# An add and a tanh-GELU over 1024 x 4096: the first load of x as eight transfers of sixteen rows

## The chip, the cores and the metric

The kernel runs on one core of a Trainium2 chip. The metric is the device time of one execution in microseconds (us), as the median of three runs. Beside it there is one profiled execution, from which every view of the profile below is taken. The profile gives times from the first instruction of the program; the span ends with the last one that it shows.

## The reference

```python
def setup_inputs():
    batch, dim = 1024, 4096
    return {"x": randn(batch, dim) as float32, "y": randn(batch, dim) as float32}

def reference(x, y):
    z = x + y
    return (0.5 * z * (1 + np.tanh(np.sqrt(2 / np.pi) * (z + 0.044715 * z ** 3)))).astype(np.float32)
```

Two arrays of 16.8 MB each are read, one of 16.8 MB is written, and every element takes one addition and one GELU. No matrix product occurs.

## The kernel before

**Layout.** The 1024 x 4096 array is viewed as 128 partitions of 8 rows each (`xv`, `yv`, `ov`, line 91), so that one partition holds 32768 consecutive floats, 128 KB. The partition is therefore the outer index of the DRAM side too: neighbouring partitions lie 128 KB apart in DRAM. The tile `zt` (line 120) holds all of x, is overwritten in place by z = x + y and at last by the result. Two buffers `y` of 8192 columns (32 KB in each partition) hold y in turn.

**Transfers.** All are issued on the SP engine's one queue. x comes in two loads of 16384 columns (`xloads`, 64 KB in each partition, 8.4 MB each), y in four loads of 8192 columns (4.2 MB each), and three stores of 16384, 10240 and 6144 columns follow. The order written out in `sp` (lines 173 to 176) is x0, y0, y1, x1, y2, y3 and then the stores. y2 may be issued only when the adds that read y0 have ended, since it takes that buffer, and y3 likewise after the adds on y1. The first store has a hand-made wait on chunk 8 (`FIRST`, line 138).

**Compute.** The columns are cut in 16 chunks of 2048. For each chunk `add` (line 149) runs on GpSimd (POOL) or on VectorE (DVE) as the table `by_dve` says; `mag` (line 154) writes the absolute value into PSUM on ScalarE (ACT); `gelu` (line 157) applies the GELU to the negated absolute value there; `end` (line 166) adds max(z, 0) on VectorE. The last is the identity gelu(z) = max(z, 0) + gelu(-|z|). The order on every engine is written out by hand (lines 173 to 211).

**Beginning and end.** After the program is compiled, `begin_early(nc, count)` takes the first `count` transfers of the SP engine out of the body and puts them ahead of the program's opening barrier, at the very head of SP's stream; with `count` 2 these are x0 and y0. It asserts that none of them waits for anything. `wait_late` lets the final barrier go on without the last store's semaphore and puts one wait for it at the end, on ScalarE.

**Semaphores of transfers.** The framework gives the transfers semaphores in turn from a set of eight (DMAHW0 to DMAHW7). The kernel before issues nine transfers: x0 has DMAHW0, y0 DMAHW1, y1 DMAHW2, x1 DMAHW3, y2 DMAHW4, y3 DMAHW5, the stores DMAHW6, DMAHW7 and, once more, DMAHW0. A transfer that takes a semaphore again waits until the earlier transfer with it has landed.

Of the kernel before, what the change touches and what calls it, by code (L numbers as in the profile page):

```python
# [8 lines left out]
def begin_early(nc, count):  # L9


    head, body = (b.instructions for b in nc.main_func.blocks[:2])
    SP = mybir.EngineType.SP
    moved = [i for i in body if i.engine == SP and isinstance(i, mybir.InstDMACopy)][:count]
    assert not any(i.sync_info and i.sync_info.on_wait for i in moved)
    assert all(i.regs_accessed() == ((), ()) for i in moved)
    at = next(k for k, i in enumerate(head) if i.engine == SP)
    for k, i in enumerate(moved):
        body.remove(i)
        head.insert(at + k, i)  # L20


def wait_late(nc):

    body, end = (b.instructions for b in nc.main_func.blocks[1:3])
    last = [i for i in body if isinstance(i, mybir.InstDMACopy)][-1]
    (sem,) = [u.id for u in last.sync_info.on_update]
    all_done = end[0]  # L30
    reset = next(i for i in end if isinstance(i, mybir.InstDrain) and i.is_reset_sema)
    at = end.index(reset)
    clear = end[at + 1]
    first, stop = reset.reset_range_start, reset.reset_range_stop
    assert all_done.engine == mybir.EngineType.SP and reset.engine == mybir.EngineType.Pool
    assert isinstance(clear, mybir.InstISA) and clear.engine == mybir.EngineType.Pool
    waits = all_done.sync_info.on_wait
    (its,) = [w for w in waits if w.id == sem]

    end[0] = mybir.InstDrain(  # L40
        name=all_done.name, engine=all_done.engine, debug=all_done.debug, is_reset_sema=False,
        sync_info=mybir.SyncInfo(on_wait=[w for w in waits if w.id != sem], on_update=[]),
    )
    parts = []
    for f, e in ((first, sem), (sem + 1, stop)):
        if f < e:
            nc.gpsimd.sem_clear(range(f, e))
            parts.append(nc.cur_bb.bb.instructions.pop())
    end[at + 1 : at + 2] = parts
    end.append(  # L50
        mybir.InstEventSemaphore(
            name=clear.name, engine=mybir.EngineType.Activation, debug=clear.debug,
            sync_info=mybir.SyncInfo(
                on_wait=[its],
                on_update=[
                    mybir.SyncUpdate(
                        sync_type="semaphore", id=sem, ant_name=its.ant_name,
                        update_mode="sem-sub-imm", update_value=its.wait_value,
                    )
                ],  # L60
            ),
        )
    )
# [3 lines left out]
def kernel(  # L67
# [11 lines left out]

    nc = tc.nc
    P = nc.NUM_PARTITIONS
    fp32 = mybir.dt.float32
# [6 lines left out]
    xv, yv, ov = (a.rearrange("(p n) d -> p (n d)", p=P) for a in (x, y, out))  # L91
# [28 lines left out]
    zt = pool_sb.tile([P, TOT], fp32, tag="z", name="z")  # L120
    yt, wt, ends = {}, {}, {}

    def load_x(i):
        a, b = xr[i]
        nc.sync.dma_start(out=zt[:, a:b], in_=xv[:, a:b])  # L125

    def load_y(i):
        a, b = yr[i]
# [45 lines left out]
    for i, (a, b) in enumerate(xr):  # L174
        sp += [(load_x, i)] + [(load_y, j) for j, (c, _) in enumerate(yr) if a <= c < b]
# [3 lines left out]
    for c in range(C):  # L179
# [6 lines left out]
            (add, c) for c in over(cr, yr[i][0] - 2 * YS, yr[i][1] - 2 * YS)  # L186
        ],
        add: lambda c: [(load_x, i) for i in over(xr, *cr[c])]
        + [(load_y, i) for i in over(yr, *cr[c])],
        mag: lambda c: [(add, c)] + ([(end, c - PS)] if c >= PS else []),  # L190
# [22 lines left out]
    ctx.close()  # L213
    tc.close()
    tc.compile()  # L215
    begin_early(nc, 2)
    wait_late(nc)


# [28 lines left out]
```

## Time and profile before

| | |
|---|---|
| median of three runs | 120.34 us (120.29 to 120.54) |
| the profiled execution's own time | 120.27 us |
| its span | 118.8 us |
| VectorE, ScalarE, GpSimd busy | 59.8, 60.8, 55.5 us |
| bytes read and written | 33.55 and 16.78 MB |

The span is 1.47 us shorter than the time of the same execution; the rest lies around it. In what follows, a "releaser" is what ended a wait; "landing" is the moment at which a transfer's semaphore has its full count; the digits of the slice rows are tenths of 40 equal slices of the span, 2.97 us each.

### The profile page before, as it was taken

The page shows a single profiled execution, that of the slowest core. Times are in us where ns is not written, and L with a number is a line of the kernel's source. Part 1 is how long each engine was busy: PE and PEld are TensorE (multiplying, and loading weights), DVE is VectorE, ACT ScalarE, POOL GpSimd, SP SyncE. Part 2 cuts the span into 40 slices and gives each one's busy share as a digit, 9 for nine tenths or more (in the row PEclk, how much of TensorE's full clock was granted, in tenths as well). Part 3 has the DMA queues.
Part 4 walks back from the last instruction along what each step waited for, and adds up shares of the span by engine and source line. Part 5 has one row for each costly group of instructions (what it writes and reads, how often), then busy time and mean ns, then how long its engine had stood idle before and what let it go on. Part 6 is the DMA issues. An engine that isn't in the chain of part 4 may idle for free.

```text
span 118.8 us, 160 instructions
## 1 busy us (share of the span) xinstructions
DVE 59.8 (50%) x24; ACT 60.8 (51%) x34; POOL 55.5 (47%) x14
## 2 busy tenths in 40 slices
DVE  0000000000399999699994595257999457742000
ACT  5000000000057989999369804797798999940000
POOL 0000000000399999998000029999999999200000
DMA  9899988989999988998899999998899889999895
GB/s 353 353 419 596 397 353 364 497 375 463 419 430 452 530 353 375 640 397 353 353 463 419 452 430 397 474 541 353 375 640 397 353 353 441 441 441 441 381 422 257
DMA packets 1296, 50.33 MB, mean 424 GB/s; under 512 B 144, under 2 KB 144, under 8 KB 144
## 3 DMA queue, kind: packets, MB, share of 16 engines
q1 hardware_dynamic: 1296, 50.33, 98.5%
HBM read 33.55 MB, written 16.78 MB: 424 GB/s over the span
## 4 chain that ended last, share of the span: by engine, by line
DMA 48%; POOL 33%; POOLq 4%; ACT 3%; DVE 2%; issue 0%; SPq 0%; DVEq 0%
DMA y<-in_y_dram 48%; POOL z L149 33%; POOLq L215 4%; DVE z L166 2%; ACT w L154 2%; ACT w L157 2%; SPq L125 0%; POOLq L149 0%; DVEq L166 0%
## 5 line engine op out<-in xcount | busy, mean ns | idle before, releaser
L149 POOL TENSOR_TENSOR z<-z,y 128x2048 f32<-128x2048 f32 x10 | 55.3, 5560 | 45.9 <-DMA y<-in_y_dram 45.9
L154 ACT ACTIVATE w<-z 128x2048 f32<-128x2048 f32 x16 | 30.1, 1880 | 42.8 <-DVE z L149 36.3
L166 DVE SCALAR_TENSOR_TENSOR z<-z,w 128x2048 f32<-128x2048 f32 (+1 forms) x17 | 36.3, 2156 | 16.0 <-ACT w L157 16.0
L149 DVE TENSOR_TENSOR z<-z,y 128x2048 f32<-128x2048 f32 x6 | 24.0, 4009 | 30.6 <-DMA y<-in_y_dram 30.6
L157 ACT ACTIVATE w<-w 128x2048 f32<-128x2048 f32 x16 | 29.8, 1862 | 0.5
L200 ACT ACT_TABLE_LOAD x1 | 1.3, 1283 | 1.3 <-PEq L232 1.3
L199 DVE MEMSET one<- 128x1 f32 x1 | 0.1, 59 | 1.3 <-PEq L232 1.3
L200 ACT ACTIVATE one<-one 128x1 f32<-128x1 f32 x1 | 0.2, 203 | 0.0
L232 POOL MEMSET const-float32-0.0<- 128x1 f32 x1 | 0.1, 99 | 0.2 <-issue 0.2
L232 POOL MEMSET const-bfloat16-1.0<- 128x1 bf16 x1 | 0.1, 102 | 0.0
L232 POOL MEMSET const-uint8-127<- 128x1 uint8 x1 | 0.1, 102 | 0.0
L232 POOL MEMSET const-float32-1.0<- 128x1 f32 x1 | 0.1, 99 | 0.0
## 6 DMA issues: line engine op xcount, KB each, us to landing
y<-in_y_dram SPq DMA_DIRECT2D x4, 4096.0 KB, 28.3
out_dram<-z SPq DMA_DIRECT2D x1, 5120.0 KB, 14.9
out_dram<-z SPq DMA_DIRECT2D x1, 3072.0 KB, 10.9
z<-in_x_dram SPq DMA_DIRECT2D x2, 40.5
out_dram<-z SPq DMA_DIRECT2D x1, 21.6
```

The lines of the kernel that those rows point to most:

```text
L149: eng.tensor_add(out=zt[:, a:b], in0=zt[:, a:b], in1=yt[s][:, o : o + b - a])
L154: nc.scalar.activation(out=wt[c], in_=zt[:, a:b], func=act.Abs)
L157: nc.scalar.activation(out=wt[c], in_=wt[c], func=act.Gelu_apprx_tanh, scale=-1.0)
L166: ins = nc.vector.scalar_tensor_tensor(out=zt[:, a + o : a + o + n], in0=zt[:, a + o : a + o + n], scalar=0.0, in1=wt[c][:, o : o + n], op ...
L199: nc.vector.memset(one, 0.0)
L200: nc.scalar.activation(out=one, in_=one, func=act.Gelu_apprx_tanh)
L215: tc.compile()
L232: nc = _bacc.Bacc("TRN2", target_bir_lowering=False, num_devices=1)
```

## The change

The load x0 of 128 partitions becomes eight loads of 16 partitions. Load j takes the partitions j, j+8, j+16, ..., j+120, each with the same 64 KB of columns as before. The second load of x is left as it was. `begin_early` now takes eight transfers to the head of SP's stream, which are these eight; y0 stays in the body, behind the opening barrier.

```diff
     def load_x(i):
         a, b = xr[i]
-        nc.sync.dma_start(out=zt[:, a:b], in_=xv[:, a:b])
+        for r in [slice(j, P, 8) for j in range(8)] if i == 0 else [slice(0, P)]:
+            nc.sync.dma_start(out=zt[r, a:b], in_=xv[r, a:b])
...
-    begin_early(nc, 2)
+    begin_early(nc, 8)
```

In the changed program's SP stream the eight loads stand first, on DMAHW0 to DMAHW7. Then come the opening barrier and y0, which takes DMAHW0 again and so waits for load 0 of x; y1 takes DMAHW1 and waits for load 1, x1 takes DMAHW2 and waits for load 2. The loads y2 and y3 and the stores keep their places and their waits on the compute engines. The first addition on each engine waits for all eight semaphores in place of two. The order of instructions on VectorE, ScalarE and GpSimd is otherwise the same.

## The prediction

> **What bounds the kernel now.** I read the slice rows first, then the list of queues, the chain, and at last stretches of the span.
>
> The page's rows for DMA (share of the 16 DMA engines, rate by slice, packets) and its queue list:
>
> ```profile
> DMA  9899988989999988998899999998899889999895
> GB/s 353 353 419 596 397 353 364 497 375 463 419 430 452 530 353 375 640 397 353 353 463 419 452 430 397 474 541 353 375 640 397 353 353 441 441 441 441 381 422 257
> DMA packets 1296, 50.33 MB, mean 424 GB/s; under 512 B 144, under 2 KB 144, under 8 KB 144
> q1 hardware_dynamic: 1296, 50.33, 98.5%
> ```
>
> The engines that move data are occupied from the first slice to the last, 98.5% of the span; no compute engine passes 51%. The packet count tells how a transfer is cut: nine transfers x 16 engines = 144 tiny packets, one semaphore update for each engine and transfer, and 1296 - 144 = 1152 = 9 x 128, so one packet for each partition row: 64 KB in x. A slice of 353 GB/s is 16 packets of 65536 bytes booked at their start in 2.97 us; the unevenness of the row is that booking.
>
> The chain that ended last, in order of time (start, length, what):
>
> ```profile
> 0.00 0.38 SPq L125
> 0.38 0.05 issue
> 0.43 31.17 DMA y<-in_y_dram
> ...
> 44.92 25.47 DMA y<-in_y_dram
> ```
>
> The chain names y, but y0 stands on the same rings behind x0, so its 31.17 us are mostly x0's. The rates of four stretches (start:end, length, engines busy, clock, DMA share, GB/s), in x0, in y0, and in both later halves:
>
> ```profile
> 3.00:20.00 17.00, 0.00 (x0) 0.00 (x0) 0.00 (x0) 1.00 1.00 432
> 22.00:31.00 9.00, 0.00 (x0) 0.00 (x0) 0.00 (x0) 1.00 1.05 451
> 42.00:60.00 18.00, 17.00 (x7) 14.86 (x9) 13.97 (x3) 1.00 1.00 431
> 80.00:98.00 18.00, 13.87 (x5) 15.91 (x10) 18.00 (x5) 1.00 0.94 408
> ```
>
> Loads at 431 to 451, whether compute runs or not: 432 / 16 = 27 GB/s for each engine, and 65536 B / 27 = 2.42 us for one row. The packet records of the trace say the same: each of 16 streams has rows of 2.418 to 2.422 us back to back, from about 1.0 us to 118.3 us, except its first, of 2.6 to 3.5 us. What each engine must move is fixed, so whatever x0 loses or gains at its engines reaches the end one for one, unless a queue runs dry, which none does now.
>
> [...]
>
> **The change part by part.**
>
> [...]
>
> *Price of x0.* Before: 8 rows x 2.42 = 19.4 us on each engine. After: 8 x 4.84 = 38.7 us. That is +19.4 us. [...] The first rows end between 3.86 and 4.66 us in the packet records, so D is 0 to 0.8; I take 0.25, -0.5. [...]
>
> *Seven more semaphore updates on each engine.* In the packet records the row after an update starts 6 ns after it. 7 x 6 = 0.04 us on the path.
>
> *Start of the first rows.* [...] Before, first packets start at 1.01 to 1.52 us. The last could start earlier by up to 0.5 us, or nothing could change; the slow engine sets the end, so -0.4 to 0. Most of it is the same lead D as above, so I count it nothing further.
>
> *The eight issues and the barrier.* Issues of loads took 0.33 to 0.50 us on SP; eight are about 3.1 us. A row takes at least 2.42 us, an issue 0.4, so the rings stay fed. The opening barrier comes some 2.3 us later (3.1 us of issues against 0.38 + 0.42), so ScalarE's table load moves from 1.26 to about 3.6. The first addition comes at 31.7, which hides it with 28 us to spare. Cost 0.
>
> *The new waits on SP.* y0 waits for load 0, which lands about 1 + 5.4 + 0.5 = 7 us; behind it stand y1 (load 1, some 12 us) and x1 (load 2, some 17 us). The rings hold x0 until about 40 us by then, 20 us by the old rate. Cost 0; y0 would have to come 13 us later than expected before an engine ran dry. The first additions' six extra waits are met long before y0 lands. y2 and y3 wait for additions which shift as a whole with y0 and y1: before, y2 was issued at 44.9, 15 us ahead of its place in the rings (x1 landed at 1.6 + 59.0 = 60.6), and that lead stays. The stores' hand-made wait shifts likewise. So nothing absorbs the loss, since compute was waiting for data, and the tail after y3 is the old one.
>
> *Sum.* +19.4 - 0.5 + 0.04 = +18.9 us. Against the profiled execution: span 118.8 + 18.9 = 137.7, plus 1.47 around it = 139.2; against the median, 120.34 + 18.9 = 139.3. I predict 139.3.
>
> **The rivals.**
>
> *The ports don't bind.* The pace is the engine's own: 27 GB/s is what an engine shows here[...]. [...] For it: the change then leaves every row at 2.42 us. [...] Then the effect is at the start: up to -0.4 us where the stagger of first packets goes, +0.04 for updates. 120.0, not slower; from -0.24 us it counts as faster. It decides as soon as the rows of x0 keep 2.42 us.
>
> [...]
>
> *Row pitch in HBM alone.* [...] No run here shows it.
>
> That the change does not do what it says is out: the order of the changed program has the eight loads at the head.
>
> **How the numbers follow.** Half the ports with even service: 0.85, from 137.8 (D = 0.8 and some start) to 141.6 [...], which holds it 0.95 of the time. Ports that don't bind: 0.08, half of it faster and half the same. Uneven service 0.04, pitch alone 0.03, both slower. 0.85 x 0.95 = 0.81, so the range is the likeliest case's own. No change means within 0.2%, 0.24 us, about what a measurement of this kernel can tell. Faster 0.04, same 0.04, slower 0.92.
>
> **What would show it.** [...] first addition at about 50.6 us rather than 31.7; y0's issue near 7 us; later stretches equal to the old, 19 us later. It is wrong if the stretch from 3 to 20 us still shows 432, or if the first addition stays at 31.7; and if the rate is halved but a stretch with idle engines follows, a wait on SP cost what I called nothing.

## The result, and the profile after

| | before | after |
|---|---|---|
| median, same chip, four runs each | 120.31 us (120.28 to 120.54) | 142.01 us (141.83 to 142.26) |
| profiled execution: time, span | 120.27, 118.8 us | 141.83, 140.1 us |

The ratio is 1.180, with a 95% interval of 1.1777 to 1.1824: 21.7 us slower. The forecast was slower, 139.3 us with a range of 137.8 to 141.6, so the direction and the place were right and the size too small by 2.7 us.

The same rows of the page as before, now of the changed kernel (share of the 16 DMA engines, rate by slice of 3.5 us, packets, queue):

```profile
DMA  9909909949938999999969699999969696899897
GB/s 299 281 19 299 299 0 299 299 94 206 299 94 356 449 449 440 412 496 393 505 299 599 299 449 440 421 430 402 552 299 599 299 599 299 374 491 444 377 407 302
DMA packets 1408, 50.33 MB, mean 359 GB/s; under 512 B 256, under 2 KB 256, under 8 KB 256
q1 hardware_dynamic: 1408, 50.33, 98.6%
```

The engines are as occupied as before (98.6% against 98.5%), and yet move 359 GB/s in place of 424. An occupied transfer engine need not be a fast one. The first twelve slices show 16 rows (299 GB/s) starting and then often a slice with nothing starting; the zeros in the DMA row come from the same booking at a packet's start. From the thirteenth slice on the rates are the old ones. The packets have grown by 112 = 7 x 16, the seven more semaphore updates on each engine: those under 512 B are 256 in place of 144.

The chain that ended last, in order of time (start, length, what):

```profile
0.00 7.98 DMA z<-in_x_dram
7.98 0.02 issue
8.00 44.90 DMA y<-in_y_dram
...
66.15 25.53 DMA y<-in_y_dram
```

y0 is now issued at 8.00, when load 0 has landed, and lands at 52.90 in place of 31.60. The second long piece is 25.53 us against 25.47 before. So everything is lost ahead of y0's landing: 21.3 us there, 21.3 us in the span.

Stretches of the changed kernel (start:end, length, three engines busy, clock, DMA share, GB/s). The first is cut so that exactly six rows of each engine start in it; the others lie in y0, x1 and the stores' part:

```profile
7.50:38.17 30.67, 0.00 (x0) 0.00 (x0) 0.00 (x0) 1.00 1.00 205
42.00:50.00 8.00, 0.00 (x0) 0.00 (x0) 0.00 (x0) 1.00 0.99 418
62.00:80.00 18.00, 17.00 (x7) 16.08 (x9) 15.18 (x3) 1.00 0.98 422
100.00:118.00 18.00, 14.12 (x6) 15.87 (x10) 18.00 (x4) 1.00 1.08 466
```

x0 runs at 205 GB/s, and what follows at full rate. In the packet records a row of 64 KB takes 5.11 us on every engine, where it took 2.42. The first stretch was made as long as six such rows, so its rate says the same as the row: 16 x 65536 B in 5.11 us are 205 GB/s.

SP's queue in the changed kernel (start, length, line, count):

```profile
0.00 5.00 SPq L127 DMA_DIRECT2D z<-in_x_dram  x8
8.00 5.45 SPq L134 DMA_DIRECT2D y<-in_y_dram  x2
18.23 0.33 SPq L127 DMA_DIRECT2D z<-in_x_dram  x1
```

y0, y1 and x1 wait as the semaphores say, yet all are issued by 18.6 us, while rows of x0 (what the prediction calls the rings are the rows that wait their turn) go on until 42.6 us. These waits cost nothing.

### The profile page after: what moved, and what is told of

Read it like the earlier page. It is cut to its first block, busy times and chain, and to the rows that moved or that the text cites. A ratio compares the mean times of both kernels' runs of the same rounds, so it can differ in the third digit from the quotient of the medians.

```text
span 140.1 us, 179 instructions
## 1 busy us (share of the span) xinstructions
DVE 59.8 (43%) x24; ACT 60.8 (43%) x34; POOL 55.5 (40%) x14
## 3 DMA queue, kind: packets, MB, share of 16 engines
q1 hardware_dynamic: 1408, 50.33, 98.6%
## 4 chain that ended last, share of the span: by engine, by line
DMA 56%; POOL 28%; POOLq 3%; ACT 3%; DVE 2%; issue 0%; DVEq 0%
DMA y<-in_y_dram 50%; POOL z L151 28%; DMA z<-in_x_dram 6%; POOLq L217 3%; DVE z L168 2%; ACT w L156 1%; ACT w L159 1%; DVEq L168 0%; POOLq L151 0%
```

## The experiments

The theory under test is that the rate of a load follows from the SBUF partitions that its rows go to. The prediction and the expectations speak of ports for this (port theory); that was an assumption, and no trace of this case shows a port. Three rivals: the rows' distance in DRAM (pitch theory), a loss at the end of every transfer (transfer theory), and the move of y0 behind the barrier with its waits. Only x0's load is edited, unless it says otherwise, and the edits are shown against the changed kernel, the last one against the kernel before. Where a version ran once, its single time stands beside the median (or the single time) of before on the same chip; the differences of time read from such runs are over 20 us.

**Sixteen neighbouring partitions.**

```diff
-        for r in [slice(j, P, 8) for j in range(8)] if i == 0 else [slice(0, P)]:
+        for r in [slice(16 * j, 16 * j + 16) for j in range(8)] if i == 0 else [slice(0, P)]:
```

> Load j of x0 takes partitions 16j to 16j+15 in place of j, j+8, ...; still eight loads of sixteen rows, rows now 128 KB apart in DRAM. Port theory: [...] a row of 64 KB takes 4 x 2.42 to 4 x 2.56 = 9.7 to 10.2 us, x0 77 to 82 us, time about 178 to 183 us. HBM pitch theory (rows 1 MB apart are what is slow): the pitch is an eighth, rows near 2.42 us, time about 120.5 us. Transfer theory (a row followed by its own semaphore update is slow, wherever it goes): rows 5.11 us as in the changed kernel, time about 142 us.

174.63 us (before 120.18). The stretch of six rows of this run:

```profile
11.00:66.30 55.30, 0.00 (x0) 0.00 (x0) 0.00 (x0) 1.00 1.00 114
```

114 GB/s, about a quarter of the full 432, and a row takes 9.22 us. A loss that grows with the rows' distance, and one that comes with each transfer's end, are both out: rows lie nearer in DRAM and the transfers are as many, and it is 33 us slower than the change. The port theory's direction holds; its size, 178 to 183, rested on an assumed fourfold row (9.7 to 10.2 us) and was a little too high.

**Near in DRAM, far in SBUF.** Load j reads sixteen neighbouring rows and writes them 8 partitions apart. The second half of x and all of y are as they were.

```diff
+            to = slice(0, P) if j is None else slice(j, P, 8)
+            of = slice(0, P) if j is None else slice(16 * j, 16 * j + 16)
-            nc.sync.dma_start(out=zt[r, a:b], in_=xv[r, a:b])
+            nc.sync.dma_start(out=zt[to, a:b], in_=xv[of, a:b])
```

> Load j of x0 reads rows 16j to 16j+15 of x, 128 KB apart in DRAM, and writes them to partitions j, j+8, ..., so x stands in other partitions than y and the output is another function of the inputs; the work is the same. Port theory: only the side of SBUF counts, rows 5.11 us, time 142 us. HBM pitch theory: rows near 2.42 us, about 120.5 us. Transfer theory: 142 us.

141.58 us (before 120.18). The stretch of six rows:

```profile
7.50:38.17 30.67, 0.00 (x0) 0.00 (x0) 0.00 (x0) 1.00 0.99 205
```

The rate of the change again, with another source layout: the side of SBUF decides. Rows take 5.085 us in place of 5.11. That half a percent can't be put down to the pitch, for the rows of the versions below that also run at 205 or 206 GB/s differ as much (5.06 to 5.12 us), and not in the order of their pitch.

**Eight loads of all partitions.** The same number of transfers, with the same waits and y0 in the same place, but cut along the columns.

```diff
-        for r in [slice(j, P, 8) for j in range(8)] if i == 0 else [slice(0, P)]:
-            nc.sync.dma_start(out=zt[r, a:b], in_=xv[r, a:b])
+        w = 2048 if i == 0 else b - a
+        for o in range(a, b, w):
+            nc.sync.dma_start(out=zt[:, o : o + w], in_=xv[:, o : o + w])
```

> x0 as eight loads of all 128 partitions and 2048 columns: the same number of transfers, semaphores and waits, the same place of y0 behind the barrier[...]. Port theory: x0 runs at 27 GB/s for each engine, 120.3 us give or take 0.6 for the beginning. HBM pitch theory: the pitch is that of before, 120.3 us. Transfer theory: eight times a loss at each transfer's end, of up to 2.7 us each, up to 142 us. If the new waits on SP were what costs, 142 us too.

120.67 us against 120.18, ratio 1.0037 (1.0023 to 1.0052), and x0 at the old rate:

```profile
5.00:19.50 14.50, 0.00 (x0) 0.99 (x2) 0.00 (x0) 1.00 1.01 426
```

Number of transfers, semaphores, waits and barrier together are worth some 0.5 us (0.3 to 0.6) of the 21.7, and the 8 KB rows, 0.309 us each or 2.47 for 64 KB, have part of it.

**Four loads of 32 partitions, 4 apart.**

```diff
-        for r in [slice(j, P, 8) for j in range(8)] if i == 0 else [slice(0, P)]:
+        for r in [slice(j, P, 4) for j in range(4)] if i == 0 else [slice(0, P)]:
...
-    begin_early(nc, 8)
+    begin_early(nc, 4)
```

> x0 as four loads of 32 partitions j, j+4, j+8, ...[...]. Port theory, [...] rows 2.42 us, 120.3 us give or take 0.6. Port theory, if an engine takes two neighbours of the list (j+8e, then j+8e+4): [...] rows 5.11 us, 142 us. [...] Transfer theory (half as many transfers): about 131 us.

120.52 us, ratio 1.0031 (1.0021 to 1.0042). The stretch in x0:

```profile
5.00:19.50 14.50, 0.00 (x0) 0.00 (x0) 0.00 (x0) 1.00 1.00 434
```

So a step in the partitions need not cost: this step of 4 over the whole range has 434 GB/s, where the step of 8 had 205. Full rate also says that an engine is not given two neighbours of the list, j+8e and j+8e+4, in that order on all engines at once, since sixteen rows j+8e are a load of the change, which ran at 205 GB/s. Already the first rows take 2.93 to 3.39 us, much as before the change (2.63 to 3.50); which engine takes which row the trace does not say. The first packets start at 1.33 to 1.65 us in place of 1.01 to 1.52, and the last row of x0 ends 0.21 us later.

**Two other sets of sixteen.** Two runs ask whether the 5.11 us belong to the step of 8. First a step of 4 inside a half of 64 (the rows of a load lie 512 KB apart in DRAM):

```diff
-        for r in [slice(j, P, 8) for j in range(8)] if i == 0 else [slice(0, P)]:
+        for r in [slice(h + j, h + 64, 4) for h in (0, 64) for j in range(4)] if i == 0 else [slice(0, P)]:
```

> x0 as eight loads of sixteen partitions with a step of 4 inside one half of 64 (j, j+4, ..., j+60, then 64 more)[...] and rows read together lie 512 KB apart[...]. Port theory: slow all the same, near 142 us. [...] rows 5.11 us, 142 us. [...] rows 4.61 us[...], x0 4 us shorter, 138 us. [...] HBM pitch theory: 120.5 us.

141.21 us (before 120.24), rows 5.06 us. Then a step of 2 inside a quarter of 32:

```diff
-        for r in [slice(j, P, 8) for j in range(8)] if i == 0 else [slice(0, P)]:
+        for r in [slice(h + j, h + 32, 2) for h in (0, 32, 64, 96) for j in range(2)] if i == 0 else [slice(0, P)]:
```

> x0 as eight loads of sixteen partitions with a step of 2 inside a quarter of 32 (j, j+2, ..., j+30)[...]. Port theory: [...] 138 to 142 us. [...] rows 4.61 us, 138 us. [...] rows 5.11 us, 142 us.

141.86 us, rows 5.11 us. The stretch of six rows in this run:

```profile
7.50:38.17 30.67, 0.00 (x0) 0.00 (x0) 0.00 (x0) 1.00 1.00 205
```

In both an engine moves 12.8 to 13.0 GB/s (65536 B in 5.11 or 5.06 us), as in the change; rows of 4.61 us, half of the 9.22 above, came in neither. The step of 8 is not what the 5.11 us belong to, for 4 inside a half and 2 inside a quarter give the same within 1%.

**The same cut in the second load of x.** x0 is whole and begins as before; x1, in the middle of the queue, is cut into partitions j, j+8, ....

```diff
-        for r in [slice(j, P, 8) for j in range(8)] if i == 0 else [slice(0, P)]:
+        for r in [slice(j, P, 8) for j in range(8)] if i == 1 else [slice(0, P)]:
...
-    begin_early(nc, 8)
+    begin_early(nc, 2)
```

> x0 whole as before, and the second load of x, which stands in the middle of the rings, in eight loads of partitions j, j+8, .... Port theory: the same price wherever the load stands: eight rows of 5.11 in place of 2.42 us, +21.5 us, and no slow first row to hide, so 120.2 + 21.3 = about 141.6 us (141 to 142.3). If instead the beginning of the program (barrier, early issue, cold engines) was what cost, 120.3 us.

142.05 us, ratio 1.1815 (1.1799 to 1.1831), the price of the change within its own spread. x0 and x1 in this run:

```profile
3.00:20.00 17.00, 0.00 (x0) 0.00 (x0) 0.00 (x0) 1.00 1.00 432
...
46.50:77.17 30.67, 19.61 (x8) 18.38 (x11) 9.48 (x2) 1.00 1.00 205
```

The cost does not come from the beginning of the program. Nor do busy compute engines change the rate: it is 205 GB/s here beside them and was 205 without them.

**The move of y0 alone.** x0 is one load, and it alone goes ahead of the barrier.

```diff
-        for r in [slice(j, P, 8) for j in range(8)] if i == 0 else [slice(0, P)]:
+        for r in [slice(0, P)]:
...
-    begin_early(nc, 8)
+    begin_early(nc, 1)
```

> x0 as one load of 128 partitions, but only that load ahead of the opening barrier, y0 behind it: the move of y0 alone. Both the port theory and the pitch theory: nothing runs dry, since y0 is issued within some 2 us and x0 occupies the rings until 21 us; 120.2 us, within 0.3. If the move of y0 costs: later, by what the engines stand idle before y0.

120.28 us, ratio 1.0002 (0.9994 to 1.0011): no change. y0 is issued at 0.79 in place of 0.43 us, and lands at 31.65 in place of 31.60.

**Two halves of 64 partitions.**

```diff
-        for r in [slice(j, P, 8) for j in range(8)] if i == 0 else [slice(0, P)]:
+        for r in [slice(0, 64), slice(64, P)] if i == 0 else [slice(0, P)]:
...
-    begin_early(nc, 8)
+    begin_early(nc, 2)
```

> x0 as two loads of 64 neighbouring partitions. [...] Port theory, rows of a load spread over all sixteen engines: [...] rows 5.11 us, 142 us. Port theory, [...] so that each load uses eight engines and both run beside each other: rows 2.42 us, 120.3 us. Transfer theory (two transfers for one): at most 2.7 us more, 123 us.

141.69 us (before 120.25), rows 5.12 us:

```profile
7.50:38.17 30.67, 0.00 (x0) 0.00 (x0) 0.00 (x0) 1.00 1.00 205
```

One cut into two neighbouring halves, without any step and with one more transfer, costs what the change costs. The two loads do not run beside each other: they land at 23.03 and 43.20 us, and the packet records have rows of some 5.12 us on all sixteen engines in both. So the two loads do not divide the engines between them, eight for each.

**A store cut the same way.** Loads as before the change; the first store goes out in eight pieces of partitions j, j+8, ..., each with the hand-made wait on chunk 8.

```diff
-        ins = nc.sync.dma_start(out=ov[:, a:b], in_=zt[:, a:b])
...
+        for r in [slice(j, P, 8) for j in range(8)] if i == 0 else [slice(0, P)]:
+            ins = nc.sync.dma_start(out=ov[r, a:b], in_=zt[r, a:b])
...
```

> Both loads of x whole as before, the first store (64 KB from each partition) in eight stores of partitions j, j+8, .... If the ports limit reading SBUF as they limit writing: rows 5.11 us, about +21.4 us, 141.7 us. If reading has more room: between 120.3 and 141 us by the rows' time. All rows of the store 1 MB apart in DRAM: a pitch effect on writes would show here too.

141.48 us (before 120.25). The stretch of six rows of the store:

```profile
84.50:115.06 30.56, 17.30 (x7) 19.47 (x11) 17.11 (x4) 1.00 0.98 206
```

Rows have a median of 5.08 us: reading these partitions of SBUF has the rate of writing them, 206 GB/s against 205.

No version here beats the kernel before: the three whose x0 keeps the full rate (434, 434 and 426 GB/s) stand at ratios of 1.0002, 1.0031 and 1.0037.

## Why the prediction was right in kind and too small

**Right: the side of SBUF.** The partitions that a load covers set its rate, and that is what the runs show. Sixteen neighbours give 114 GB/s; sixteen with a step of 8, of 4 inside a half or of 2 inside a quarter, and 64 neighbours, give 205, and a store with the step of 8 gives 206; all 128 and 32 with a step of 4 over the whole range give 426 to 434. The DRAM side (205 with rows 128 KB apart), the number of transfers (426 in eight loads of all partitions) and the place in the queue (205 in x1) do not move that. By what rule a set of partitions comes to its rate no run shows.

**Wrong: the term "8 x 4.84 = 38.7 us".** That a row of the change takes twice 2.42 us ("half the ports" in the prediction's odds) was the author's assumption, and no trace of before showed it. Measured, each engine moves 12.8 GB/s, 5.11 us for a row, so x0 is 8 x 5.11 = 40.9 us: 2.2 of the 2.7 us that were missing. The upper end of the range, 141.6 us, rested on an assumption as well, and lies short of the measured 142.0. Why a row takes 5.11 us and not 4.84 no run shows.

**The lead, -0.5 us, was too generous.** That a lead D of one engine over another shortens x0 was the author's assumption. Measured, the fourth row takes 5.01 to 5.11 us, the fifth 4.89 to 5.00 and the last 5.04 to 5.11, against 5.11: 0.2 to 0.3 us came back, 0.28 on the engine that ended x0 last. Whether a lead is the cause no run shows.

**The start, counted nothing, costs.** First packets start at 1.37 to 1.98 us, where before had 1.01 to 1.52: 0.4 us later, not earlier. The bound -0.4 to 0 had the wrong sign. Against it stands a gain that I did not see: before, the first row was slow on every engine (2.6 to 3.5 us against 2.42), and now that disappears in the longer row (4.2 to 5.1).

The engine that ended x0 last, by the packet records: start 1.52 to 1.98 (+0.46), first row 3.14 to 5.13 (+1.99), rows two to eight 16.91 to 35.49 (+18.58), in all +21.03. Its first row thus grew by 0.7 us less than the 2.69 us of a later row. The first rows of y0 have the remaining 0.26 of the 21.29 us at its landing: they take 1.35 to 2.00 us in place of 1.21, while the last rows of x0 end (41.30 to 42.61 us); the cause was not tested. So the span's miss, 140.1 us for a forecast of 137.7, is made of +2.2 for the rows, +0.2 for the lead, +0.46 for the start, +0.26 for y0 and -0.7 for the first row. That the rows' term alone comes near the whole is partly luck, for the others nearly cancel. The remaining 0.3 us lie around the span, 1.73 us in place of 1.47.

**Costs put at nothing or nearly.** The seven semaphore updates, the waits of y0, y1 and x1, and the barrier were rightly called small: the eight loads of all partitions have them all and cost some 0.5 us. Eight issues took 5.00 us, not 3.1, and ScalarE's table load began at 5.65, not 3.6; with the first addition at 52.9 that has no effect. y0 was issued at 8.00 for an expected 7.

**The rivals.** That every engine keeps its own pace of 27 GB/s, the pitch and uneven service of the engines are refuted: by the neighbouring partitions (7.1 GB/s for each engine), by the run that is near in DRAM (205 GB/s as with far rows), and by rows of equal length on all engines (5.10 to 5.12 us for the second and third). One reading of the lines was loose: the rows of 2.42 us are those of 64 KB alone, and y's rows of 32 KB took 1.21 us, at the same rate.

## What to carry to other kernels

When transfers bound a kernel, look at which partitions are in flight at one moment, not only at how many transfers or bytes. A cut along the partitions into sixteen neighbours (9.22 us for a row in place of 2.42), halves (5.12) or a step of 8 (5.11) doubled the load's time here or worse, and a step of 8 did the same to a store (5.08). A cut along the columns (426 GB/s) or by a step of 4 over the whole range (434) kept the rate. A share of occupied engines near 100% does not show this (98.6% here at 359 GB/s, 98.5% before at 424); compare the rate of a stretch with that of another stretch of the same kernel.

## What the hardware showed beyond this

The three rates are not simple parts of one another. A row of 64 KB took 2.42, 5.11 and 9.22 us, so an engine moved 27.1, 12.8 and 7.1 GB/s: the second row is 2.11 times as long as the first, and the third 1.80 times as long as the second. What sets the 27.1 no run shows.

At the head of the stream, the length of an issue on SP went with the shape of the transfer: 0.38 us for x0 whole, 0.42 for sixteen neighbouring partitions, 0.59 for sixteen with a step of 8, 4 or 2, 0.55 to 0.58 for 64 neighbours. Shape is not all: of the eight pieces of the store, the first two took 0.56 and 0.57 us to issue and the others 2.60 to 2.68, and no run shows why. First packets followed: from 1.02 us after sixteen neighbours, from 1.37 us after a step of 8. Smaller first transfers did not start the engines earlier here than x0 whole, which had its first packets from 1.01 us.
